# Moving two kinds of weight load from SyncE's queue to GpSimd's, with new places and delays, in a one-core decoder layer

## The chip, the cores and the metric

One core of a Trainium2 chip runs the whole kernel in one launch. The metric is the device time in microseconds (us), lower being better. TensorE multiplies matrices, VectorE (DVE) and ScalarE (ACT) do elementwise work, GpSimd (POOL) does a few small things here, and SyncE (SP) asks for most transfers. Each engine works through its own instructions in order. A DMA can be asked for on SP's queue or on POOL's; those that add to what lies at their destination are asked for on POOL's.

## The reference

A decoder layer over 256 tokens of width 2048 in float32:

```python
hn = rmsnorm(h, norm_mix_w)
q, k, v, g_ret, xr, yr, g_a, g_b = split(hn @ w_in)            # 2048 x 14336
ret_out = silu(g_ret) * head_groupnorm(chunkwise_retention(rotary(q), rotary(k), v))
rnn_out = gelu(yr) * rg_lru(causal_dwconv(xr))
merged = sigmoid(g_a) * (ret_out @ w_proj_ret) + sigmoid(g_b) * (rnn_out @ w_proj_rnn)
h = h + merged @ w_mix_out
h = h + memory_cross_attention(rmsnorm(h), rmsnorm(mem), w_q, w_k, w_v, w_o)
h = h + (silu(gate) * val) @ w_down        # gate, val = causal_dwconv(rmsnorm(h) @ w_up), 2 x 5632
out = rmsnorm(h, final_norm_w)
```

## The kernel before

**Products.** Every product is made in parts: a float32 operand is split into a high part, rounded to a shorter format that TensorE takes at full pace, and a low part, the rest. A product is then three matmuls, high x high, low x high and high x low. The high part of a weight is a ScalarE copy (`weight_parts`, L451), the low part a VectorE subtraction (L452).

**The weight stream.** The host lays all weights in one array in the order of use, and the kernel walks it piece by piece (`weight_stream`, 358 pieces, numbered by `i`). `plan` lists the weight products in order. A plain one covers 512 output columns, with a piece of four 128-row blocks. A pair covers two times 512 columns, with a piece of two row blocks by two column blocks (1 MB). `prefetch` loads a piece on SP into one of three buffers `raw` and splits it; `AHEAD = 2` keeps two pieces prepared ahead of the one in TensorE. `chunks` hands out a piece, counts a step per piece, and then runs the work that `later(n, fn)` put off by n steps.

**Kinds of pieces in a pair.** `MARKS` names for each pair the places (0 to 7, two row blocks each) that are treated in another way than the plain two-by-two product (kind 0). The numbers in a pair's tuple mean: 1 to 9, and 20s by their last digit, use seven block products instead of eight (Strassen's scheme, `steps_pair`), for which sums of the weight blocks and of the activations are needed; 20s also have their weight sums begun by DMA; -11 to -17 have lower parts of half of the piece (place 1 to 7) made by DMA, and -1 to -9 those of the whole piece.
- Kind 1, seven products: `seven_parts` makes the weight sums on VectorE with one addition of 1024 columns and two of 512 (L473).
- Kind 4, seven products with double loads: `load_twice` asks for one block twice into a tile `tw`, `add_to` lets a DMA on POOL's queue add two other blocks to it (L330), and `seven_loaded` has two VectorE additions of 512 columns left (L337).
- Kinds 2 and 3, far pieces: `request` loads blocks into a tile `fr`, `subtract` has ScalarE write their negation, rounded, into `fl` (L319) and a DMA on POOL's queue add the float32 block to it (L320), so that VectorE has no subtraction for these; kind 3 does so for half of the piece.

`LAG` says how many pieces ahead these begin: `far_load=3` and `sum_load=4` for the loads, 0 for ScalarE's negation and the additions; and how many steps other work is put off: `gelu` for the step from a transposed block to gelu (`gelu_y`), `rnn` and `rnn_step` for the activation sums of `w_proj_rnn`, `heads` for the split of the retention heads, `two_heads` for the heads' transposes, `residual` for squares, `key_turn` for the second pair of key blocks in the attention.

**Order.** Matmuls are kept in program order. For the other instructions a scheduler orders each engine's instructions by program order and by when their inputs are expected; it also gives out the 31 buffers of the pool `big`, in which `tw`, `fr`, `fl` and most activations live. An instruction waits in its engine's queue until its inputs are there and its buffer is free, and what is behind it on that engine waits too.

**Transposes.** Row blocks are turned into column blocks by DMA transposes asked for on SP (`by_dma`), followed `wait` steps later by ScalarE copies that join the halves (L677) and by whatever comes next.

Of the kernel before, what the change touches and what calls it, by code (L numbers as in the profile page):

```python
# [17 lines left out]
P = 128  # L18
D = 2048
S = 256  # L20
NT = D // P
# [5 lines left out]
FF = 5632  # L27
NF = FF // P
BW = 512
KC = 4  # L30
KH = 2
# [3 lines left out]
WARM = 7  # L35
FREE = 300
LAG = dict(
    sums=3, two_heads=3, recur=3, gelu=6, merged=4, memory=1, memory_step=4, rnn=2, rnn_step=2,
    heads=2, heads_step=1, squares=2, squares_step=1, rows=17, rows_step=2, residual=5, gate=2,
    value=4, merge_turn=1, query_turn=2, key_turn=3, turn=3, attend=3, acc_m=0, acc_h=0,  # L40
    by_rotate=0, by_conv=0, by_gelu=1, by_attend=1, far=0, far_load=3, sum_load=4, sum_add=0,
)
EPS = 1e-6
GN_EPS = 1e-5
# [1 line left out]
EARLY = [2, 2, 4, 4, 4]  # L46
MARKS = [
# [11 lines left out]
O_Q, O_K, O_V, O_G = 0, 1024, 2048, 4096  # L59
O_XR, O_YR, O_GA, O_GB = 6144, 8192, 10240, 12288  # L60
# [139 lines left out]
def hybrid_layer(  # L200
# [17 lines left out]
    act, dve, pe, pool, sp = nc.scalar, nc.vector, nc.tensor, nc.gpsimd, nc.sync  # L218
# [15 lines left out]
    def big(shape, dt=F32, s="b"):  # L234
        return bp.tile(shape, dt, tag="big", name=nm(s))
# [19 lines left out]
    def load(out, in_, pin):  # L255
        i = sp.dma_start(out=out, in_=in_)
        if pin:
            tc.keep_in_program_order(i)
# [43 lines left out]
    def source(i):  # L302

        _, _, nk, c = stream[i]
        return wall[at[i - 1] : at[i]].rearrange("(p k n) -> p k n", p=P, k=2 * nk if isinstance(c, tuple) else nk)

    def request(i):

        far[i] = []
        for k in (0, KH)[: 2 if stream[i][3][2] == 2 else 1]:  # L310
            raw = big([P, KH, BW], s="fr")
            load(raw, source(i)[:, k : k + KH, :], False)
            far[i].append(raw)

    def subtract(i):
# [7 lines left out]
    def load_twice(i):  # L323

        far[i] = t = big([P, KH, BW], s="tw")
        load(t, source(i)[:, 3:4, :].to_broadcast([P, KH, BW]), False)

    def add_to(i):

# [210 lines left out]
    def gemm_n(*args):  # L540
        return ended(steps_n(*args))
# [98 lines left out]
    def pair(*args):  # L640
        return ended(steps_pair(*args))

    def paired():

        return isinstance(plan[gemms[0]][3], tuple)
# [280 lines left out]
    for g in range(2):  # L926
        dec = big([P, 4, S], s="dec")
        vs, turned = [], ([], [])
        for b, o in enumerate((O_Q, O_K)):

            def rotate_both(f, o=turned[b]):
                o.append(rotated(f[:, 0:2, :]))
                later(0, lambda: o.append(rotated(f[:, 2:4, :])))

            v = None
            if b and not g and paired():
                a, v = pair("w_in", 0, xs, NT, O_K, O_V + BW)
                scaled(a, rs0)
                by_dma(a, rotate_both)
            else:  # L940
                a = gemm_n("w_in", 0, xs, NT, o + g * BW) if g + b else q0
                turned_rows(a, rs0, rotate_both, 2 - b if g + b else 3, g + b > 0, LAG["by_rotate"])
            if b == 1:
                sp.dma_start(
                    out=dec,
                    in_=consts[:, C_DEC + g * 4 * S : C_DEC + (g + 1) * 4 * S].rearrange("p (h s) -> p h s", s=S),
                )
            if g == 0:
                if v is None:
                    v = gemm_n("w_in", 0, xs, NT, O_V + b * BW) if b else ended(v_steps)  # L950
                vs.append(split_rows(v, rs0))
        if g == 1:
            vs += [split_rows(v, rs0) for v in pair("w_in", 0, xs, NT, O_V + 1024, O_V + 1024 + BW)]
        qr, kr = turned
        gates = []
        c = O_G + g * 1024
        for a in pair("w_in", 0, xs, NT, c, c + BW):
            t = big([P, 2, BW], s="gate")
            for tt in range(2):
                act.activation(t[:, tt, :], a[:, tt, :], AF.Silu, scale=rs0[:, tt : tt + 1])  # L960
            gates.append(t)
        retain(g, qr, kr, vs, dec, gates)
# [137 lines left out]
    def turn_merged(f):  # L1100
        for pr in range(2):
# [6 lines left out]
            if len(merged) == 2:  # L1108
                for k2 in range(NT // 2):
                    later(LAG["memory"] + LAG["memory_step"] * k2, lambda k2=k2: ms[k2])  # L1110

    ts, mb = [], []
    for b in range(2):
        ts.append(tanh_rows(big([P, 2, BW], s="sig"), gemm_n("w_in", 0, xs, NT, O_GB + b * BW)))
# [2 lines left out]
                later(LAG["rnn"] + LAG["rnn_step"] * i, lambda k2=k2: sums_of(rnn[k2]))  # L1117
    for b in (0, 2):
        if b:
            ts = [tanh_rows(a, a) for a in pair("w_in", 0, xs, NT, O_GB + b * BW, O_GB + (b + 1) * BW)]  # L1120
        for t, z in zip(ts, pair("w_proj_rnn", 0, rnn, NT, b * BW, (b + 1) * BW)):
            gated(t, z)
            mb.append(z)
# [3 lines left out]
        later(LAG["squares"] + LAG["squares_step"] * c, lambda c=c: memory_squares(c))  # L1127
    ts = []
    for b in (0, 2):
        ts += [tanh_rows(a, a) for a in pair("w_in", 0, xs, NT, O_GA + b * BW, O_GA + (b + 1) * BW)]  # L1130
    later(3, memory_begun)
    for b in range(4):
        later(LAG["rows"] + LAG["rows_step"] * b, lambda b=b: hrow.append(load_rows(x, b)))
# [169 lines left out]
    def down(b0, hid, n):  # L1303

        for b in (0, 2):
            for i, z in enumerate(pair("ffn_w_down", b0 * BW, hid, n, b * BW, (b + 1) * BW)):
                pool.dma_start(out=hrow[b + i], in_=z, accum_op=ALU.add)

    def down_final(b0, hid, n):
# [85 lines left out]
    def up(b, hid, seven, wait):  # L1395

        gt, vl = (big([P, 4, S], s=a) for a in ("fg", "fv"))

        def by_two(fn):
            fn(0)  # L1400
            if b < NF // 4 - 1:
                later(0, lambda: fn(1))
            else:
                fn(1)

        def gate(f):
            by_two(lambda pr: conv(f, 4 * b, gt, pr))

        def value(f):

            def both(pr):
                conv(f, NF + 4 * b, vl, pr)
                gate_up(gt, vl, hid, seven, pr)

            by_two(both)

        two = pair("ffn_w_up", 0, h2s, NT, b * BW, FF + b * BW)
        for a, then, wait in zip(two, (gate, value), (LAG["gate"], wait)):
            with tc.high_priority(FREE):
                for tt in range(2):  # L1420
                    act.mul(a[:, tt, :], a[:, tt, :], rs2[:, tt : tt + 1])  # L1421
            by_dma(a, then, wait)
# [58 lines left out]
```

## Time and profile before

| | before |
|---|---|
| median of 3 runs | 1954.9 us (1953.95 to 1956.12) |
| profiled execution, its own time | 1956.59 us |
| its span, first to last instruction | 1954.5 us |
| granted TensorE clock, mean | 0.999 |
| HBM read | 407.27 MB |
| packets of SP's queue, share of 16 engines' span | 66.5% |
| packets of POOL's queue, the same | 6.3% |

The profiled execution is one run; its span goes from the first instruction to the last, and its own time is somewhat longer. PE is TensorE's matmuls, PEld its weight loads beside them. A "SPq" or "POOLq" is the queue part of an engine: it asks for DMAs. In lists of groups the columns are busy us and mean ns of one, then the idle time before them and what ended it.

### The profile page before, as it was taken

To read this page: it belongs to the slowest core of one execution; us is meant where nothing else is said; L and a number is where in the kernel's file an instruction comes from. 1 tells how busy PE (TensorE), PEld (TensorE's weight loads), DVE (VectorE), ACT (ScalarE), POOL (GpSimd) and SP (SyncE) were. 2 spreads that over 40 slices of the span, in tenths; PEclk is the share of its full clock that TensorE was granted. 3 is DMA by queue.
4 is the path that set the end of the run, shared out by engine and by line. 5 is a ranking of instruction groups with operands and counts; after the bars stand their busy time and mean duration, and the time that the engine had idled before them with its cause. 6 is when DMAs were issued, how large, how long until landed. Compare 5 with 4: busy or idle time off the path is not lost.

```text
span 1954.5 us, 24287 instructions
## 1 busy us (share of the span) xinstructions
PE 1944.4 (99%) x8735; PEld 1612.9 (83%) x8735; DVE 1659.0 (85%) x2155; ACT 1457.7 (75%) x1792; POOL 68.5 (4%) x69
## 2 busy tenths in 40 slices
PE   9999999999999999999999999999999999999998
PEld 7888888888888888888888888888887888888887
DVE  6887987787889988887888857789999889999986
ACT  6665758999756666778678777888877578884784
POOL 0000001000100000000000000000000000000000
PEclk9999999999999999999999999999999999999999
DMA  8866767666867786778868687676677877678773
GB/s 332 262 215 198 245 222 217 213 218 229 237 217 265 233 264 215 253 253 252 247 213 239 223 221 225 226 232 226 211 224 224 269 248 221 223 224 271 230 255 119
DMA packets 211352, 454.99 MB, mean 233 GB/s; under 512 B 143264, under 2 KB 147872, under 8 KB 170400
## 3 DMA queue, kind: packets, MB, share of 16 engines
q1 hardware_dynamic: 204896, 430.38, 66.5%
q0 software_dynamic: 6336, 23.07, 6.3%
q8 instruction: 68, 1.11, 0.2%
q14 instruction: 52, 0.43, 0.1%
HBM read 407.27 MB, written 2.10 MB: 209 GB/s over the span
## 4 chain that ended last, share of the span: by engine, by line
PE 88%; DVE 5%; ACT 3%; DMA 2%; issue 2%; POOL 0%; SPq 0%; POOLq 0%; DVEq 0%; ACTq 0%
PE acc L285 63%; PE sm L285 26%; DVE lo L452 2%; ACT hi L451 1%; DMA raw<-in_wall 1%; ACT f L677 1%; DVE o L627 1%; ACT pl L664 0%; DMA fl<-fr 0%; DVE o L638 0%; DMA pt<-pl 0%; DVE raw L473 0%; DVE fv L1282 0%; DVE fg L1282 0%; DVE s L702 0%
## 5 line engine op out<-in xcount | busy, mean ns | idle before, releaser
L452 DVE TENSOR_TENSOR lo<-raw,hi 128x1024 fp32r<-128x1024 f32 (+1 forms) x824 | 940.4, 1169 | 203.0 <-ACT hi L451 193.0
L285 PE MATMUL acc<-hi,s 128*128 128x512 f32 x3526 | 1081.5, 388 | 0.4 <-ACT s L727 0.2
L451 ACT CAST hi<-raw 128x1024 fp32r<-128x1024 f32 (+1 forms) x824 | 801.1, 1007 | 301.9 <-DMA raw<-in_wall 83.1
L285 PEld LDWEIGHTS acc<-hi,s 128*128 128x128 f32 x3526 | 659.5, 188 | 136.1 <-DVE s L728 0.6
L285 PE MATMUL acc<-lo,s 128*128 128x512 f32 x1727 | 669.7, 388 | 0.1
L285 PE MATMUL sm<-hi,s 128*128 128x512 f32 x1464 | 450.9, 389 | 0.0
L285 PEld LDWEIGHTS acc<-lo,s 128*128 128x128 f32 x1727 | 324.4, 188 | 68.6 <-DVE lo L452 2.1
L285 PEld LDWEIGHTS sm<-hi,s 128*128 128x128 f32 x1464 | 274.7, 188 | 57.2 <-ACT prob L1203 0.2
L285 PE MATMUL sm<-lo,s 128*128 128x512 f32 x720 | 280.3, 389 | 0.0
L677 ACT COPY f<-pt 128x1024 uint16<-128x1024 uint16 x128 | 166.8, 1353 | 10.0 <-DMA pt<-pl 10.0
L285 PEld LDWEIGHTS sm<-lo,s 128*128 128x128 f32 x720 | 135.2, 188 | 28.6 <-DVE lo L452 0.6
L285 PE MATMUL acc<-hi,ts 128*128 128x512 f32 x438 | 134.9, 389 | 0.0
L473 DVE TENSOR_TENSOR raw<-raw 128x1024 f32<-128x1024 f32 x147 | 127.1, 865 | 1.9
L285 PEld LDWEIGHTS acc<-hi,ts 128*128 128x128 f32 x438 | 82.2, 188 | 17.0
L285 PE MATMUL acc<-lo,ts 128*128 128x512 f32 x219 | 85.7, 391 | 0.7 <-DVE lo L452 0.6
L664 ACT COPY pl<-o 128x1024 uint16<-128x1024 uint16 x64 | 62.5, 1040 | 3.7 <-DVE o L638 2.8
L330 POOL DMA_DIRECT2D tw<-in_wall x24 | 21.4, 891 | 980.8 <-DMA tw<-in_wall 355.7
L285 PEld LDWEIGHTS acc<-lo,ts 128*128 128x128 f32 x219 | 41.1, 188 | 10.8 <-DVE lo L452 2.4
L664 ACT COPY pl<-rows 128x1024 uint16<-128x1024 uint16 x44 | 43.7, 1044 | 7.6 <-DVE rows L694 7.6
L1421 ACT ACTIVATE o<-o,ro 128x512 f32<-128x512 f32 x44 | 30.1, 718 | 23.9 <-DVE o L638 23.8
L638 DVE TENSOR_TENSOR o<-o,sm 128x512 f32<-128x512 f32 x64 | 42.2, 679 | 3.9 <-PE sm L285 3.9
L285 PE MATMUL sm<-hi,ts 128*128 128x512 f32 x146 | 45.0, 389 | 0.0
(197 smaller groups left out, 1321.2 us busy)
## 6 DMA issues: line engine op xcount, KB each, us to landing
raw<-in_wall SPq DMA_DIRECT2D x319, 1024.0 KB, 5.1
raw<-in_wall SPq DMA_DIRECT2D x24, 768.0 KB, 5.6
tw<-in_wall SPq DMA_DIRECT2D x24, 512.0 KB, 7.7
tw<-in_wall POOLq DMA_DIRECT2D x24, 512.0 KB, 7.3
raw<-in_wall SPq DMA_DIRECT2D x13, 512.0 KB, 6.6
fr<-in_wall SPq DMA_DIRECT2D x12, 512.0 KB, 7.4
fl<-fr POOLq DMA_DIRECT2D x12, 512.0 KB, 8.1
nat<-in_x SPq DMA_DIRECT2D x8, 512.0 KB, 9.7
```

What stands on the lines that cost most here:

```text
L285: tc.keep_in_program_order(pe.matmul(*a, **k))
L330: pool.dma_start(out=far[i], in_=source(i)[:, 0:KH, :], accum_op=ALU.add)
L451: act.copy(hi[:, cs], src[:, cs])
L452: dve.tensor_tensor(out=lo[:, cs], in0=src[:, cs], in1=hi[:, cs].bitcast(F32), op=ALU.subtract)
L473: dve.tensor_tensor(out=o, in0=a, in1=b, op=ALU.add)
L627: dve.tensor_tensor(out=o, in0=a, in1=b, op=op)
L638: dve.tensor_tensor(out=o, in0=o, in1=a, op=ALU.add)
L664: act.copy(planes[:, tt], words[:, tt])
L677: act.copy(halves_[:, :, :, cs], turned_[:, :, :, cs])
L1421: act.mul(a[:, tt, :], a[:, tt, :], rs2[:, tt : tt + 1])
```

## The change

The loads of `request` and `load_twice` are asked for on POOL's queue instead of SP's. In `MARKS`, the pair `w_proj_rnn` columns 0 to 1023 has place 3 (piece 93) no longer with double loads but with VectorE's sums, and place 5 (piece 95) without a part made by DMA; the pair `w_in` for the gate `g_b`, columns 1024 to 2047, has place 7 (piece 105) without one. Several delays are set anew. A helper `blocks` gives a pair's two blocks as `pair` does, or two plain products where a pair has no seven; it takes the place of `pair` in five places.

```diff
 LAG = dict(
-    sums=3, two_heads=3, recur=3, gelu=6, merged=4, memory=1, memory_step=4, rnn=2, rnn_step=2,
-    heads=2, heads_step=1, squares=2, squares_step=1, rows=17, rows_step=2, residual=5, gate=2,
-    value=4, merge_turn=1, query_turn=2, key_turn=3, turn=3, attend=3, acc_m=0, acc_h=0,
-    by_rotate=0, by_conv=0, by_gelu=1, by_attend=1, far=0, far_load=3, sum_load=4, sum_add=0,
+    sums=3, two_heads=2, recur=3, gelu=7, merged=4, memory=1, memory_step=4, rnn=3, rnn_step=1,
+    heads=3, heads_step=2, squares=2, squares_step=1, rows=17, rows_step=2, residual=4, gate=2,
+    value=4, merge_turn=1, query_turn=2, key_turn=5, turn=3, attend=3, acc_m=0, acc_h=0,
+    by_rotate=0, by_conv=0, by_gelu=3, by_attend=2, far=0, far_load=3, sum_load=4, sum_add=0,
+    by_up=1,
 )
 MARKS = [
...
-    ((22, 23, 24, -16, -15, -11), (2, 5, 6, -17, -11), (2, 3, 5),),
+    ((3, 22, 24, -16, -11), (2, 5, 6, -11), (2, 3, 5),),
...
     def request(i):
...
-            load(raw, source(i)[:, k : k + KH, :], False)
+            pool.dma_start(out=raw, in_=source(i)[:, k : k + KH, :])
...
     def load_twice(i):
         far[i] = t = big([P, KH, BW], s="tw")
-        load(t, source(i)[:, 3:4, :].to_broadcast([P, KH, BW]), False)
+        pool.dma_start(out=t, in_=source(i)[:, 3:4, :].to_broadcast([P, KH, BW]))
...
+    def blocks(w, row, st, nk, c1, c2):
+        if paired():
+            yield from ((a, True) for a in pair(w, row, st, nk, c1, c2))
+        else:
+            for c in (c1, c2):
+                yield gemm_n(w, row, st, nk, c), False
...
-        two = pair("ffn_w_up", 0, h2s, NT, b * BW, FF + b * BW)
-        for a, then, wait in zip(two, (gate, value), (LAG["gate"], wait)):
+        two = blocks("ffn_w_up", 0, h2s, NT, b * BW, FF + b * BW)
+        for (a, own), then, wait in zip(two, (gate, value), (LAG["gate"], wait)):
+            if not own:
+                turned_rows(a, rs2, then, wait, by=LAG["by_up"])
+                continue
```

More of the change, by code (lines that the diff above doesn't have):

```diff
@@ L952, in hybrid_layer @@
         if g == 1:
-            vs += [split_rows(v, rs0) for v in pair("w_in", 0, xs, NT, O_V + 1024, O_V + 1024 + BW)]
+            vs += [split_rows(v, rs0) for v, _ in blocks("w_in", 0, xs, NT, O_V + 1024, O_V + 1024 + BW)]
         qr, kr = turned
@@ L956, in hybrid_layer @@
         c = O_G + g * 1024
-        for a in pair("w_in", 0, xs, NT, c, c + BW):
+        for a, _ in blocks("w_in", 0, xs, NT, c, c + BW):
             t = big([P, 2, BW], s="gate")
@@ L1110, in turn_merged, with tanhs @@
                     later(LAG["memory"] + LAG["memory_step"] * k2, lambda k2=k2: ms[k2])
+    def tanhs(c):
+        for a, own in blocks("w_in", 0, xs, NT, c, c + BW):
+            yield tanh_rows(a if own else big([P, 2, BW], s="sig"), a)
     ts, mb = [], []
@@ L1119, in hybrid_layer @@
         if b:
-            ts = [tanh_rows(a, a) for a in pair("w_in", 0, xs, NT, O_GB + b * BW, O_GB + (b + 1) * BW)]
+            ts = list(tanhs(O_GB + b * BW))
         for t, z in zip(ts, pair("w_proj_rnn", 0, rnn, NT, b * BW, (b + 1) * BW)):
@@ L1129, in hybrid_layer @@
     for b in (0, 2):
-        ts += [tanh_rows(a, a) for a in pair("w_in", 0, xs, NT, O_GA + b * BW, O_GA + (b + 1) * BW)]
+        ts += tanhs(O_GA + b * BW)
     later(3, memory_begun)
@@ L1305, in down @@
         for b in (0, 2):
-            for i, z in enumerate(pair("ffn_w_down", b0 * BW, hid, n, b * BW, (b + 1) * BW)):
+            for i, (z, own) in enumerate(blocks("ffn_w_down", b0 * BW, hid, n, b * BW, (b + 1) * BW)):
+                if not own:
+                    a, z = z, big([P, 2, BW], s="o")
+                    with tc.high_priority(FREE):
+                        act.copy(z, a)
                 pool.dma_start(out=hrow[b + i], in_=z, accum_op=ALU.add)
@@ L1415, in value @@
             by_two(both)
-        two = pair("ffn_w_up", 0, h2s, NT, b * BW, FF + b * BW)
-        for a, then, wait in zip(two, (gate, value), (LAG["gate"], wait)):
+        two = blocks("ffn_w_up", 0, h2s, NT, b * BW, FF + b * BW)
+        for (a, own), then, wait in zip(two, (gate, value), (LAG["gate"], wait)):
+            if not own:
+                turned_rows(a, rs2, then, wait, by=LAG["by_up"])
+                continue
             with tc.high_priority(FREE):
```

## The prediction, made before the change was run

> **What bounds the kernel now.** I read the page's first part, then the stretches of 50 us with TensorE's matmul counts, then the chain of work that ended last, and only then the queues that the change touches.
>
> ```profile
> span 1954.5 us, 24287 instructions
> PE 1944.4 (99%) x8735; PEld 1612.9 (83%) x8735; DVE 1659.0 (85%) x2155; ACT 1457.7 (75%) x1792; POOL 68.5 (4%) x69
> 1108.24 54.43 PE acc L285 x240
> 500.00:550.00 50.00, 49.37 (x219) 1.00 0.86 260
> 550.00:600.00 50.00, 50.00 (x222) 1.00 0.55 193
> 800.00:850.00 50.00, 49.87 (x220) 1.00 0.80 260
> 1450.00:1500.00 50.00, 49.53 (x214) 1.00 0.69 217
> 1500.00:1550.00 50.00, 49.62 (x218) 1.00 0.80 260
> ```
>
> TensorE is busy 99% of the span. A busy share alone could hide stalls, so I take the pace: the third line, from the chain, has 240 products in 54.43 us with nothing between them, 0.2268 us each. At that pace 50 us hold 220 starts, and a stretch counts one or two more that lie over its edges: 222 is a full stretch (second column: us, third: PE busy, in brackets the matmuls). Four stretches in the middle are short by 3, 2, 8 and 4 matmuls, 17 x 0.2268 = 3.9 us together. That is all that this change could win back, for it touches neither the first loads nor the last product, and it leaves every product in place: in all the pairs the set of second-level positions that use seven products instead of eight is the same before and after (the order in the tuple differs in one). 3.9 us is 0.2% of the time, about what a measurement of this kernel can tell from no change. The kernel is at its floor: the question is whether the change brings new gaps, not how much work it saves.
>
> **The change part by part.** First the calls. `blocks` yields what `pair` yields wherever a pair's marks name a seven, and all pairs that now go through it have one, so it and `by_up` change nothing. `by_gelu` and `by_attend` are only asked whether they are zero, so 3 for 1 and 2 for 1 change nothing.
>
> Second, the loads that move from SP to POOL.
>
> ```profile
> tw<-in_wall SPq DMA_DIRECT2D x24, 512.0 KB, 7.7
> tw<-in_wall POOLq DMA_DIRECT2D x24, 512.0 KB, 7.3
> fr<-in_wall SPq DMA_DIRECT2D x12, 512.0 KB, 7.4
> fl<-fr POOLq DMA_DIRECT2D x12, 512.0 KB, 8.1
> L256 SPq DMA_DIRECT2D tw<-in_wall x24: 378/426/1374, 81.5 to 1793.2; - x24
> L330 POOL DMA_DIRECT2D tw<-in_wall x24: 865/880/1054, 89.1 to 1799.7; - x24
> L256 SPq DMA_DIRECT2D fr<-in_wall x12: 327/382/1139, 214.6 to 1263.7; - x12
> SPq L256 <- DVE lo L452: 1209.9, 300, 11.9
> ```
>
> The first four lines give size and time to landing, the next three the least, median and most ns of one issue. SP loses 24 x 0.426 + 12 x 0.382 = 14.8 us of issuing. None of it is on the path: SP stood 1209.9 us waiting for VectorE's split to free a weight buffer (last line), and the waits, not the issues, place the weight loads. POOL gets 23 double loads and 10 far loads (one and two fewer, from the marks). A load on POOL is not in this trace; the nearest row is POOL's own 0.88 us for the accumulating load of the same tile and size, which lands after 7.3 us against SP's 7.7, so 33 x 0.88 = 29 us on an engine that is busy 4%. Bounds for one: 0.4 us earlier to 0.5 us later (0.880 less 0.382). The cover is the lead. A double load is asked for four pieces ahead of the preparation and the preparation runs two pieces ahead of the products: six pieces of about 5.2 us, 31 us, against 7.7 + 7.3 for load and addition. I cost the move at nothing, with 13 us or more to spare for a double load after the split's 1 to 2 us.
>
> The far loads have less: three plus two pieces, 26 us, against 7.4 for the load, 1.06 for ScalarE's negation and 8.1 for the addition, 17 us. 9 us are left. This is where POOL's order counts: an addition waits on POOL for its load to land or for ScalarE, and now the next load can stand behind it, where SP used to send it past.
>
> Third, the places. Two pieces (numbered by the order of the weight stream: 95 and 105) stop having lower parts made by DMA; piece 93 makes its weight sums on VectorE alone again.
>
> ```profile
> L452 DVE TENSOR_TENSOR lo<-raw,hi 128x1024 fp32r<-128x1024 f32 x745 | 889.4, 1220 | 199.5 <-ACT hi L451 189.7 <-PE acc L285 4.2 <-PE sm L285 2.1
> L473 DVE TENSOR_TENSOR raw<-raw 128x1024 f32<-128x1024 f32 x49 | 59.8, 1219 | 0.5
> L319 ACT ACTIVATE fl<-fr 128x1024 fp32r<-128x1024 f32 x12 | 12.6, 1056 | 0.0
> 500.00:520.00 20.00, 19.37 (x86) 15.73 (x85) 16.33 (x28) 12.30 (x16) 1.75 (x2) 1.00 0.88 263
> 520.00:540.00 20.00, 20.00 (x89) 16.54 (x89) 16.37 (x20) 14.76 (x17) 1.74 (x2) 1.00 0.80 223
> 560.00:580.00 20.00, 20.00 (x90) 16.57 (x89) 17.85 (x22) 12.42 (x14) 0.87 (x1) 1.00 0.61 202
> 580.00:600.00 20.00, 20.00 (x90) 16.57 (x89) 19.06 (x25) 13.55 (x17) 0.15 (x1) 1.00 0.62 236
> ```
>
> Each far piece given up returns one subtraction of 1.22 us to VectorE and takes 1.06 us from ScalarE and one addition from POOL; piece 93 takes one addition of 1024 columns back, 1.22 us. VectorE +3.66 us, ScalarE -2.1 us. In the window rows the busy times run PE, PE load, DVE, ACT, POOL. For 93 and 95 VectorE has 3.7 us idle in each 20 us (16.33, 16.37), against 2.44 in all; 105 is prepared at about 575, where 2.15 and 0.94 us are idle, against 1.22. On the path: nothing, with 0 to 3.7 us as the bounds.
>
> Fourth, the delays. The one with a gap next to it is `gelu` 6 to 7.
>
> ```profile
> 491.05 2.56 ACT L677 COPY f<-pt 128x1024 uint16<-128x1024 uint16 x2
> 494.93 1.06 ACT L1066 ACTIVATE f<-f 128x1024 f32<-128x1024 f32 x1
> 497.79 1.14 ACT L701 CAST s<-rn 128x512 fp32r<-128x512 f32 x2
> 499.50 1.29 DVE s L702 x2
> 503.16 0.97 ACT fl L319
> 504.52 8.56 DMA fl<-fr
> 513.12 2.56 PE acc L285 x10
> PE acc L285 <- DMA fl<-fr: 0.6, 1, 0.6
> 504.52 0.88 POOL L320 DMA_DIRECT2D fl<-fr  x1 [10.34 <-ACT fl L319]
> 518.47 0.87 POOL L320 DMA_DIRECT2D fl<-fr  x1 [13.08 <-ACT fl L319]
> ```
>
> This is the short stretch at 512. TensorE waits for the lower part of piece 91, which landed 8.56 us after POOL asked at 504.52, and POOL stood idle 10.34 us for ScalarE's negation. Ahead of it in program order ScalarE had the last gelu block (copies, table load, gelu, two casts, 491.05 to 498.9) and VectorE that block's split and the sums that ScalarE then waited for. One step later puts the gelu block behind the preparation of piece 91: a step is one piece, and the preparation of 91 falls in the step between. ScalarE then has about 6 us less in front of the negation, the addition can land before 513.1, and the gap goes: 0.63 us of PE idle, 3 matmuls by the count, 0.7 us. Next in line is that block's own output, wanted at pieces 96 and 97, five pieces later, with more than 20 us to spare. `rnn` and its step put the sums for piece 92 about one piece later, still some 6 us ahead of TensorE. The others (`two_heads`, `heads`, `residual`) move work inside leads of five pieces or more; I cost them at nothing. `key_turn` is a rival, below.
>
> The other short stretches (820, 1450 to 1540) are not reached by any delay. There SP loses one or two issues of 0.43 us; I credit nothing.
>
> **Sum.** The profiled execution took 1956.59 us for a span of 1954.5, 2.1 around it, and lies 1.7 above the median of the three runs, 1954.9. 1956.6 - 0.7 = 1955.9 for that execution, so 1954.2 for the median. The case's own range is 1951.0 (all 3.9 us come back) to 1958.6 (the 3.7 us of VectorE's extra work all on the path): within 0.2% either way.
>
> **Rivals.** *Slower by POOL's order.* In the stretch around 500 us the code asks POOL, in this order, for load 91, load 92, load 94, negated addition 91, addition 92, load 96, addition 94, load 99, addition 96. Load 96 used to go out on SP; now it stands behind two waiting additions. For: POOL's two longest waits there are the quoted 10.34 and 13.08 us. One of them in front of a far load uses up its 9 us and leaves 1.3 us of gap, both leave 23.4 - 9 = 14.4. It decides from 9 us of waiting. Between those ends I take 8 us, half-way: 1963. Against: the additions' waits are mostly for ScalarE, which gets freer here.
>
> *Slower by the delay of the keys.* `key_turn` 3 to 5 joins and splits the second pair of keys two steps later.
>
> ```profile
> 1086.60 0.64 ACT L701 CAST s<-f 128x512 fp32r<-128x512 f32 x1
> 1102.49 5.75 PE sm L285 x48
> 1080.00:1100.00 20.00, 20.00 (x89) 16.42 (x89) 20.00 (x23) 16.87 (x21) 0.00 (x0) 1.00 0.69 262
> ```
>
> The last split began at 1086.6; two pieces, 10.4 us, put it at 1097, its VectorE half at about 1098. The 48 products are the two logits, so those keys are wanted half-way, at 1105.4: 7 us left of 18. But VectorE is busy all of 1080 to 1100 and the products behind it wait as well. From 7 us of backlog on it opens a gap: behind the weight splits of two more pieces (10.4 us) it is 3.4 us, behind three 8.6; the middle, 6, gives 1960. Against: the same work leaves room in 1070 to 1087.
>
> *Slower by starved issues.* If POOL could write its requests only while VectorE is idle (3.7 of 20 us at 500), 0.88 us would become 4.8; five issues in front of load 96 are then 19.4 us late, 10 more than the lead: 1965. The rows speak against it: with VectorE busy 85%, POOL's issues took 865 to 1054 ns. The Trainium skill, SBUF — State Buffer, section "SBUF: two separate sides", has such a rule: requests from GpSimd's queue are written by GpSimd through a port pair that VectorE locks in its two-port modes, and it advises the hardware queues instead. It gives about 620 ns alone against 3100 beside a VectorE copy; by that, five issues are an estimated 12 us late and the time about 3 us longer. This trace shows no such issue, and VectorE's work here is two-input arithmetic almost throughout.
>
> *Faster beyond 0.2%.* SP, rid of 14.8 us of issues, sends the weight loads earlier and all four short stretches close: 1951 or just below.
>
> ```profile
> 1445.14 6.93 DMA raw<-in_wall
> 1474.13 5.88 DMA raw<-in_wall
> ```
>
> For: these two, from the chain, stand before the short stretch at 1450 to 1500. Against: what the loads waited for was a free buffer, not an issue.
>
> **How the numbers follow.** Forecast (the 512 gap goes, nothing else opens) 0.52; POOL's order 0.24; keys 0.15; starved issues 0.03; all gaps closed 0.06. So faster by over 0.2% is 0.06, within 0.2% is 0.52, slower by over 0.2% is 0.42. The range runs from 1951.0 to 1965.0, which takes in the middle of each slower case; what is left out, some 0.15 to 0.2, is the upper half of POOL's order and the little below 1951.
>
> **What would show it.** Right: a stretch 500 to 550 with 222 matmuls and no PE wait for fl; 23 double and 10 far loads under POOLq at about 0.9 us each; VectorE's busy time up by some 3.7 us, ScalarE's down by 2. Wrong: matmul counts below 222 anywhere new; in 500 to 550 with POOL idle in front of far loads (POOL's order), around 1105 with TensorE waiting for a key's split (keys), or POOL issues of several us (starved). Far off would be a change in the matmuls' number, or a gap at a place that I did not weigh, through buffers freed in another order.

## The result, and the profile after

The changed kernel is slower: 1968.9 us, median of 7 runs (1964.9 to 1980.29), against 1954.97 for the kernel before in the same session, a ratio of 1.0076 with a 95% interval of 1.0063 to 1.0088. The forecast was 1954.2 and its range ended at 1965.0.

The profiled execution of the changed kernel took 1980.29 us for a span of 1978.5. It is the longest of the seven, so what it shows is at the upper end of what this kernel does. These are the first lines of its page and of its queues.

```profile
span 1978.5 us, 24282 instructions
PE 1949.3 (99%) x8735; PEld 1613.0 (82%) x8735; DVE 1660.8 (84%) x2158; ACT 1452.5 (73%) x1790; POOL 86.9 (4%) x99
tw<-in_wall POOLq DMA_DIRECT2D x46, 512.0 KB, 7.5
fr<-in_wall POOLq DMA_DIRECT2D x10, 512.0 KB, 5.5
```

The matmuls are the same 8735. The 46 requests for `tw` are 23 double loads and 23 additions. The stretches of 50 us come next, with the columns as in the prediction, so the matmuls are in brackets and the last three numbers are the granted clock, the DMA share and GB/s.

```profile
500.00:550.00 50.00, 50.00 (x222) 1.00 0.68 221
650.00:700.00 50.00, 48.12 (x210) 1.00 0.60 212
800.00:850.00 50.00, 50.00 (x222) 1.00 0.79 263
1100.00:1150.00 50.00, 50.00 (x245) 1.00 0.76 227
1150.00:1200.00 50.00, 34.69 (x142) 0.83 0.84 126
1450.00:1500.00 50.00, 49.49 (x214) 1.00 0.80 232
1500.00:1550.00 50.00, 49.80 (x218) 1.00 0.72 230
```

The stretch at 500 is full now. One stretch is new and large: 1150 to 1200 has 80 matmuls less than a full 222, which at 0.2268 us each is 18.1 us. In it the DMA engines are busier (0.84) than in the other stretches shown and move 126 GB/s against their 212 to 263. A smaller hole is at 650 (12 matmuls, 2.7 us). TensorE's waits name the large one, in total us, times and longest:

```profile
PE acc L286 <- ACT ps L1254: 12.6, 1, 12.6
PE acc L286 <- DVE lo L453: 2.7, 6, 0.8
PE acc L286 <- DVE ps L1255: 2.7, 1, 2.7
```

`ps` is the split of the attention's probabilities (L1254 its high part on ScalarE, L1255 its low part on VectorE), which the next attention product needs. The wait for `fl` is gone from this list. The chain of work around the hole shows what stood ahead of `ps`:

```profile
1119.92 34.01 PE acc L286 x150
...
1154.34 23.70 DMA pt<-pl
1178.04 0.02 issue
1178.06 1.34 ACT f L686
...
1187.70 0.61 DVE ps L1255
1188.31 0.04 issue
1188.35 5.03 PE acc L286 x13
```

A DMA transpose of the attention's rows, asked for at 1154.34, landed 23.7 us later. The last line adds something: 13 products took 5.03 us, 0.387 each instead of 0.2268, 2.1 us more. The granted clock of that stretch is 0.83 in the mean, and from 1180 to 1192 it is 0.50. So 15.3 us of waiting and 2.1 us of slow products make up most of the hole of 18.1.

ScalarE's timeline shows the link from the transpose to `ps` (start, us, what, and in brackets the idle time before it and what ended it):

```profile
1169.37 1.35 ACT L686 COPY f<-pt 128x1024 uint16<-128x1024 uint16 x1 [9.42 <-DMA pt<-pl]
1178.06 1.33 ACT L686 COPY f<-pt 128x1024 uint16<-128x1024 uint16 x1 [7.34 <-DMA pt<-pl]
...
1183.80 0.62 ACT L1254 CAST ps<-f 128x512 fp32r<-128x512 f32 x1
```

The two copies that join the halves wait 9.42 and 7.34 us for the two transposes, and everything behind them on ScalarE waits too, `ps` last. Before, the same two copies began at 1158.84 without a wait and `ps` at 1165.81.

What ran beside those transposes? First the kernel before, POOL's timeline of 1140 to 1185 and then SP's:

```profile
1142.28 0.87 POOL L330 DMA_DIRECT2D tw<-in_wall  x1 [83.67 <-DMA tw<-in_wall]
1161.85 0.89 POOL L330 DMA_DIRECT2D tw<-in_wall  x1 [18.70 <-ACT f L677]
1167.27 0.88 POOL L330 DMA_DIRECT2D tw<-in_wall  x1 [4.54 <-ACT v L716]
```

```profile
1151.58 5.16 SPq L665 DMA_TRANSPOSE pt<-pl  x2
1156.79 0.58 SPq L256 DMA_DIRECT2D tw<-in_wall  x1
1158.75 0.33 SPq L256 DMA_DIRECT2D raw<-in_wall  x1
1159.24 0.38 SPq L256 DMA_DIRECT2D tw<-in_wall  x1
```

Then the changed kernel, the same two views (x2 is two issues in a row, with the time from the first to the last one's end):

```profile
1141.92 0.74 POOL L327 DMA_DIRECT2D tw<-in_wall  x1 [28.13 <-PE acc L286]
1147.75 0.87 POOL L331 DMA_DIRECT2D tw<-in_wall  x1 [5.09 <-DMA tw<-in_wall]
1149.98 0.76 POOL L327 DMA_DIRECT2D tw<-in_wall  x1 [1.36 <-ACT s L710]
1155.72 0.86 POOL L331 DMA_DIRECT2D tw<-in_wall  x1 [4.98 <-DMA tw<-in_wall]
```

```profile
1152.57 8.07 SPq L674 DMA_TRANSPOSE pt<-pl  x2
```

In POOL's views L331 (L330 before) is an addition and L327 a double load. They come in the order of the pieces of the pair `xa_w_o`, 212, 215 and 216; 1142.28 before is 212's addition, and the views after begin with 215. Before, SP's one queue put the double loads of 215 and 216 behind the pair of transposes (1151.58, then 1156.79 and 1159.24), and so their additions came after the pair had landed. After the change both go out on POOL ahead of the pair: 215 at 1141.92 with its addition at 1147.75, and 216 at 1149.98 with its addition at 1155.72, in the middle of the pair. The pair and this addition land late: the transposes after 16.8 and 23.7 us, the addition after 22.9. The load of 216 itself landed in time, after 5.4 us. Over the whole kernel the landing of a transpose (least, median, most) was 3.0, 3.3 and 7.7 us before; the view of the tile `pt` after has:

```profile
DMA to landing us min/median/max: 3.0/3.8/23.7
```

### The profile page after: what moved, and what is told of

Its sections match the earlier page's. It is cut to its first block, busy times and chain, and to the rows that moved or that the text cites. A ratio compares the mean times of both kernels' runs of the same rounds, so it can differ in the third digit from the quotient of the medians.

```text
span 1978.5 us, 24282 instructions
## 1 busy us (share of the span) xinstructions
PE 1949.3 (99%) x8735; PEld 1613.0 (82%) x8735; DVE 1660.8 (84%) x2158; ACT 1452.5 (73%) x1790; POOL 86.9 (4%) x99
## 4 chain that ended last, share of the span: by engine, by line
PE 89%; DMA 3%; DVE 3%; ACT 2%; issue 1%; POOL 0%; SPq 0%; POOLq 0%; DVEq 0%; ACTq 0%
PE acc L286 62%; PE sm L286 27%; DMA pt<-pl 2%; DMA raw<-in_wall 1%; DVE lo L453 1%; ACT hi L452 1%; ACT f L686 0%; ACT pl L673 0%; DVE s L711 0%; DVE fv L1296 0%; DVE raw L474 0%; DVE tb L858 0%; ACT rows L926 0%; DMA raw<-in_head 0%; ACT fg L1294 0%
## 5 line engine op out<-in xcount | busy, mean ns | idle before, releaser
L628 DVE TENSOR_TENSOR o<-o,acc 128x512 f32<-128x512 f32 x64 | 43.6, 681 | 0.5
```

The costliest lines, as they stand in the source:

```text
L628: dve.tensor_tensor(out=o, in0=a, in1=b, op=op)
```

## The experiments

All times are medians with the range of the runs, and each ratio is against the kernel before, run in the same session on the same chip.

**Which part of the change costs.** The first: the changed kernel with both kinds of load back on SP, so that only places and delays differ from before.

```diff
 def request(i):
-            pool.dma_start(out=raw, in_=source(i)[:, k : k + KH, :])
+            load(raw, source(i)[:, k : k + KH, :], False)
 def load_twice(i):
-        pool.dma_start(out=t, in_=source(i)[:, 3:4, :].to_broadcast([P, KH, BW]))
+        load(t, source(i)[:, 3:4, :].to_broadcast([P, KH, BW]), False)
```

> The changed kernel with both kinds of loads asked for on SP again; its places and delays stay. Theory Q (the loads on POOL's queue cost it): the time falls to 1953 to 1956, no transposed block lands later than about 10 us, no gap of TensorE over 2 us in the middle. Theory D (the new delays and places cost it): 1963 to 1975 as with the change, with the gap before the attention's last blocks near 1171 us.

Measured: 1956.08 (1954.9 to 1958.42), ratio 1.0001 (0.9991 to 1.001). Two of its 50 us stretches, for comparison with those above:

```profile
650.00:700.00 50.00, 50.00 (x222) 1.00 0.67 213
1150.00:1200.00 50.00, 50.00 (x222) 1.00 0.76 212
```

Both holes are gone. The second run is the opposite: the kernel before with these two lines changed as the diff of the change has them, and nothing else.

> The kernel before with both kinds of loads asked for on POOL; its places and delays stay. Theory Q: slower by 8 us or more, 1963 to 1975, with transposes or additions that land after 15 us or more somewhere. Theory D: 1953 to 1957.

Measured: 1968.79 (1957.79 to 1972.22), ratio 1.006 (1.0041 to 1.0078); TensorE waits 4.9 and 2.7 us for `ps`. The third has only the double loads back on SP (the second half of the diff above), with the far loads on POOL.

> The changed kernel with only the double loads back on SP, the far loads left on POOL. Theory Q with the double loads as the part that counts (256 descriptors of 2 KB, 23 of them): 1953 to 1957. If the far loads count: 1960 or more. Theory D: 1963 to 1975.

Measured: 1957.21 (1954.89 to 1959.65), ratio 1.0006 (0.9997 to 1.0016). The fourth is the changed kernel again, unaltered.

> The changed kernel unchanged, for a second profile of it. If its extra time is one fixed gap (the attention blocks at 1171 us, 15 us of idle TensorE), the gap is there again in the same place. If it is a collision of transfers that depends on small shifts, the large gap is elsewhere, of another size, or absent, and the times spread over 1963 to 1980 again.

Measured: 1969.7 (1968.97 to 1971.68), ratio 1.0071 (1.0056 to 1.0086). Its waits show that the hole is in the same place but varies in size from one execution to the next, so neither theory holds as it stood:

```profile
PE acc L286 <- DVE ps L1255: 3.1, 1, 3.1
...
PE acc L286 <- ACT ps L1254: 1.7, 1, 1.7
```

What follows: places and delays cost and gain nothing that can be measured, the far loads on POOL about 1 us, which is within the noise, and the double loads on POOL nearly all of it.

**Which double loads.** The changed kernel has 23: 3 in `xa_w_o`, 6 in the feed-forward products, 14 elsewhere. First the three of `xa_w_o` go back to SP.

```diff
-        pool.dma_start(out=t, in_=source(i)[:, 3:4, :].to_broadcast([P, KH, BW]))
+        (sp if stream[i][0] == "xa_w_o" else pool).dma_start(out=t, in_=source(i)[:, 3:4, :].to_broadcast([P, KH, BW]))
```

> The changed kernel with the double loads of one pair alone (xa_w_o, pieces 212, 215, 216) back on SP, the other 20 left on POOL. Theory P (one place: there POOL sends a double load and its addition past the transposes of the attention's rows, which on SP stood ahead of the load): the gap near 1170 us goes and the time falls by 7 to 10 us, to 1958 to 1962. Theory W (every double load on POOL costs a little): it falls by 3 of 23 parts, 2 us.

Measured: 1963.95 (1962.1 to 1968.61), ratio 1.0046 (1.0031 to 1.0061), and no wait for `ps`. The fall of some 5 us lies between the two theories. Then those of the feed-forward products as well (`or stream[i][0].startswith("ffn")` added to the condition).

> The changed kernel with the double loads of xa_w_o and of the feed-forward products (11 of 23) on SP, 12 left on POOL. If what is left beside the gap at 1170 us lies in the feed-forward part (late weights at 1450 to 1560 us): 1956 to 1959. If it is spread over all: 1960 to 1962.

Measured: 1960.21 (1957.11 to 1963.29), ratio 1.0022 (1.0012 to 1.0031). By its trace this run has 9 double loads on SP and 14 on POOL; the expectation's 11 and 12 were miscounted. So the loss goes in steps: 1.0071 with all on POOL, 1.0046, 1.0022, 1.0006 with all double loads on SP, 1.0001 with the far loads there too. In us of 1955.4 the steps are 4.9, 4.7, 3.1 and 1.0; neighbouring intervals touch, so the order of size is not settled between the first three. The large hole is one of several meetings.

The other way round, the kernel before with only the three of `xa_w_o` on POOL (the same line, with `!=`):

> The kernel before with the double loads of xa_w_o alone asked for on POOL. Theory P: the gap near 1170 us appears, with transposes that land after 12 us or more, and the time rises by 6 to 10 us, to 1961 to 1965. Theory W: by 2 us.

Measured: ten runs in two groups, five of 1954.81 to 1957.39 and five of 1969.55 to 1972.7; ratio of the medians 1.0035 (1.001 to 1.0061). The median, 1963.47, is inside the expected range only because it lies between the groups. The profiled run is of the upper group. Its POOL timeline:

```profile
1140.40 0.75 POOL L326 DMA_DIRECT2D tw<-in_wall  x1 [26.61 <-DMA pt<-pl]
1146.34 0.88 POOL L330 DMA_DIRECT2D tw<-in_wall  x1 [5.19 <-DMA tw<-in_wall]
1149.70 0.74 POOL L326 DMA_DIRECT2D tw<-in_wall  x1 [2.48 <-ACT hi L451]
1154.85 0.90 POOL L330 DMA_DIRECT2D tw<-in_wall  x1 [4.40 <-DMA tw<-in_wall]
```

These are load and addition of piece 215, then of 216. The pair went out on SP from 1151.81, 216's addition at 1154.85 in the middle of it, and TensorE waited 9.3 + 2.7 us for `ps`. Three loads make the whole hole in a kernel that is otherwise the one before, and they make it all or nothing: about 15 us in half of the runs.

**Is it the loads themselves?** Two kernels without the layer, which only ask for these transfers again and again, with nothing else going on. The first puts a pair of transposes behind one other transfer, or two.

```python
sections = (
    lambda i: [turned(i)],
    lambda i: [twice(sp, i), turned(i)],
    lambda i: [twice(pool, i), turned(i)],
    lambda i: [added(i), turned(i)],
    ...
)
```

> Not the layer: a pair of DMA transposes of the kernel's size, twelve times each alone and just behind a double load on SP, a double load on POOL, an addition on POOL, a 1 MB weight load on SP, and that weight load with each of the three; then each of the three alone. If a transfer on POOL's queue as such slows transposes (theory Q): the second transpose of the pair lands 2 us or more later behind a double load on POOL than behind one on SP. If only the moment counts, that is that SP used to hold the load back behind the transposes (theory P): the same within 1 us. If additions are what jams: the section with weight load and addition has transposes of 10 us and more.

Measured, medians from the first request of a pair to its last landing: alone 4.43 us, behind a double load of SP 5.76, of POOL 6.57, behind an addition 6.88, with a 1 MB weight load as well 7.90, 8.02 and 8.16; the longest of all 9.18. A double load on POOL is 0.8 us worse for the pair than one on SP, which is within theory P's 1 us, and nothing comes near 20 us. An addition that is asked for ahead of the pair does not jam it here.

The second has the kernel's sequence: weight load, pair, weight load on SP, and a double load with its addition, which waits for it.

```python
def chain(engine, i, first, add=True, second=True):
    ...
    if first:
        made.append(twice(engine, i))
    made.append(raw(i))
    made.append(turned(i))
    ...
    if add:
        add_to(made[0 if first else 2], i)
```

> Not the layer: the transfers around the gap at 1170 us by themselves, 24 times each: a weight load, a pair of transposes and another weight load on SP, with a double load on POOL or SP ahead of the pair or behind it and its addition on POOL once it has landed. Theory J (two POOL transfers, the load's end and the addition, that meet a pair of transposes jam them): in the sections with the double load ahead the pair's second transpose lands after 12 us or more in some of the 24, and with the load behind the pair never. Theory T (it needs the whole kernel's traffic): all pairs land within 9 us, and the sections differ by 1 to 2 us at most.

Measured, the same medians: double load ahead on POOL 6.6 (7.6 without the addition), ahead on SP 12.3 (9.7 without), behind the pair on SP 6.3. Asked for behind the pair on POOL, where nothing holds it back, the load in fact went out 1.2 us ahead of the pair: 7.8. With the load ahead on POOL the addition was asked for 5.0 us after the pair's first request, when the pair was nearly done (landings at 5.7 and 6.6). With the load ahead on SP it was asked for at 5.9, when the second transpose without an addition lands only at 9.7, and the two landed together at 12.3. So theory J's 12 us came in all 24 turns with the load ahead on SP and in none with it on POOL; a load ahead on SP delays the pair by itself, and an addition that starts inside the pair adds 2.6 us there. The 17 to 24 us of the layer are not reached.

**Moving the moment.** Three runs of the changed kernel. In the first, ScalarE's join of the attention's rows comes one step later, so that `ps` is no longer right behind it.

```diff
-        turned_rows(a, shares[b], lambda f: split_block(f, osp, marks_of("xa_w_o")), by=LAG["by_attend"])
+        turned_rows(a, shares[b], lambda f: split_block(f, osp, marks_of("xa_w_o")), 2, by=LAG["by_attend"])
```

> The changed kernel with the join of the attention's turned row blocks put off one step more (2 for 1). If the late transpose costs time because ScalarE's join of it stands in order ahead of the probabilities' copy that TensorE needs next, the wait for ps near 1170 us goes, though the transposes still land after 12 us or more, and the time falls by 6 to 10 us. If TensorE loses the time to late weights instead, it stays at 1966 to 1972.

Measured: 1970.48 (1962.46 to 1976.68), ratio 1.0068 (1.0048 to 1.0089). No better: TensorE still waited 5.1 us for `ps` in the profiled run. The remedy at the waiting end does not work. The second has the double loads one piece later (`sum_load=3`), on POOL.

> The changed kernel, loads on POOL, with every double load asked for one piece later (sum_load 3 for 4, some 5 us). Theory M (the moment counts: on POOL the loads go out ahead of the transposes and weight loads that SP kept in front of them): the gap at 1170 us goes or changes, and the time falls to 1957 to 1963. Theory Q (POOL's queue as such): 1966 to 1972 as with the change.

Measured: 1982.83 (1977.13 to 1988.31), ratio 1.0134 (1.0111 to 1.0158): slower than either theory said. The waits for `ps` are 11.3 + 2.7 us, and a transpose lands after 22.9 us at most; both additions, 215's and 216's, now start inside the pair. Later loads give other meetings, not fewer. The third has them one piece earlier (`sum_load=5`) and on SP.

> The loads on SP again and every double load asked for one piece earlier (sum_load 5 for 4). Theory M: a load that stands ahead of the transposes on SP costs as well, 1959 or more. Theory Q: 1954 to 1957, like the loads on SP with 4.

Measured: 1957.3 (1955.56 to 1959.34), ratio 1.0008 (0.9998 to 1.0017). This does not test theory M at the attention's pair: by the trace the loads of 215 and 216 went out at 1155.30 and 1156.43, still behind the pair on SP (1149.99).

**Holding POOL's requests.** Four runs on what decides at 1150 to 1190. The kernel before with the three loads of `xa_w_o` on POOL (the one with two groups), and one addition held: between the load and the addition of piece 215 POOL copies two elements of the rows that the attention's pair of transposes writes.

```diff
 def add_to(i):
+        if stream[i][0] == "xa_w_o" and stream[i][1] == 1280:
+            gate = sp_.tile([P, 2], U16, tag="gate", name=nm("gate"))
+            with tc.issue_after(loaded[i].ins):
+                behind_turn = pool.tensor_copy(gate, turns[-2][:, 0, 0, 127:129])
+            with tc.issue_after(behind_turn.ins):
+                pool.dma_start(out=far[i], in_=source(i)[:, 0:KH, :], accum_op=ALU.add)
+            return
         pool.dma_start(out=far[i], in_=source(i)[:, 0:KH, :], accum_op=ALU.add)
```

> The kernel before with the three double loads of xa_w_o on POOL (as in the run where the times fell into two groups, 1954.8 to 1957.4 and 1969.6 to 1972.7), and one addition held: POOL copies two elements of the attention's turned rows to a scratch tile between the load and the addition of piece 215, so that this addition can't start before those two transposes have landed. Theory S (an addition that starts while a pair of transposes is in flight makes both land late): the pair lands within 9 us, no wait of TensorE near 1170, all runs in 1954 to 1958. Theory Q (any double load on POOL beside the transposes does it, through its bytes or its queue): still two groups, the upper at 1970 or more.

Measured: 1957.02, all eleven runs within 1953.3 to 1957.66, ratio 1.0 (0.9991 to 1.0008). No run is in the upper group. The run with two groups was of another session and chip, so this sets 0 of 11 against 5 of 10 across sessions. POOL's timeline, SP's, and the landing of the transposes from 1140 to 1192:

```profile
1156.82 0.42 POOL L335 COPY gate<-pt 128x2 uint16<-128x2 uint16 x1 [17.92 <-DMA pt<-pl]
1157.38 0.88 POOL L337 DMA_DIRECT2D tw<-in_wall  x1
1158.22 0.80 POOL L326 DMA_DIRECT2D tw<-in_wall  x1
1167.01 0.90 POOL L339 DMA_DIRECT2D tw<-in_wall  x1 [7.99 <-DMA tw<-in_wall]
```

```profile
1149.44 5.21 SPq L675 DMA_TRANSPOSE pt<-pl  x2
```

```profile
DMA to landing us min/median/max: 4.0/5.2/6.4
```

The landing went from 20.4 us at most to 6.4. But the hold moves more than one addition, since what stands behind the copy on POOL waits with it. The addition of 215 goes from 1146.34 to 1157.38, and the load and the addition of 216, the two that had met the pair (1149.70 and 1154.85), go to 1158.22 and 1167.01. The load of 215 had landed at 1144.40, 5 us before the pair was asked for. So the run shows that the hole goes when POOL's requests stay clear of the pair. It does not part the load of 216 from its addition, as it was meant to do with 215's. The next run holds the load of 215 as well, with the copy ahead of it.

> As the first, but the copy stands ahead of the load of piece 215 on POOL, so that load and addition both start after the two transposes have landed. Theory S and theory Q: 1954 to 1958, all runs in one group. If this is in one group and the run with only the addition held is in two, the load does it. If neither is in one group, POOL's queue as such is at fault, or another piece.

Measured: 1957.7 (1955.89 to 1961.39), ratio 1.0008 (0.9999 to 1.0017). Holding the load of 215 (now at 1159.06) adds nothing; 216 is behind the pair in both runs. The next has one double load only, that of piece 215, on POOL.

```diff
-        load(t, source(i)[:, 3:4, :].to_broadcast([P, KH, BW]), False)
+        (pool if stream[i][0] == "xa_w_o" and stream[i][1] == 1280 else sp).dma_start(out=t, in_=source(i)[:, 3:4, :].to_broadcast([P, KH, BW]))
```

> The kernel before with one single double load, that of piece 215, on POOL; all other loads on SP. Theory S: one load is enough, since its addition then starts beside the pair: two groups, 1954 to 1958 and 1966 to 1973. If it needs the other two loads as well (more bytes on POOL): one group, 1954 to 1957.

Measured: 1959.29 (1955.89 to 1964.57), ratio 1.0012 (1.0003 to 1.0021), one group and barely clear of the noise. The two groups that the theory expected did not come. The profiled run's POOL timeline, with the load and the addition of 215, says why:

```profile
1142.18 0.77 POOL L326 DMA_DIRECT2D tw<-in_wall  x1
1150.39 0.88 POOL L330 DMA_DIRECT2D tw<-in_wall  x1 [7.44 <-DMA tw<-in_wall]
```

In the two-group run it was 216 whose load and addition met the pair. Here 216's load is on SP again and goes out behind the pair, at 1158.79. The addition of 215 started 0.3 us before the pair was asked for (1150.69). The pair's transposes then took 9.0 and 7.6 us and TensorE waited 0.9. So 215 alone does not make the large hole, and an addition already in flight cost little in this execution.

Last, the changed kernel with the same hold; 216's load and addition again come behind it (1165.66 and 1174.05).

> The changed kernel with the same one addition (piece 215) held behind the attention's transposes, all loads on POOL. Theory S: the gap of TensorE near 1171 goes, the smaller gaps elsewhere (650, 1450 to 1560) stay, 1961 to 1965. Theory Q: 1968 to 1971 as without it.

Measured: 1966.32 (1963.53 to 1969.59), ratio 1.0048 (1.0035 to 1.006). There is no wait for `ps` left; the median is above the expected 1961 to 1965. In the median this one place is worth about 3 to 5 us (1.0071 to 1.0048 here, to 1.0046 with the three loads on SP). The remaining 9 us is spread, as the waits of its profiled run show:

```profile
PE acc L286 <- DVE lo L462: 3.2, 6, 1.2
PE sm L286 <- DVE o L648: 2.3, 2, 2.1
```

The first line is of weight splits that came late. The hole at 650 in the changed kernel reads so: POOL sends two double loads (631.14, 639.40) and two additions (640.54, 643.82) around three weight loads, which land after 9.8 to 11.1 us; with the loads on SP weight loads there land after 4.7 to 6.9. That these meetings make the small holes is read from the trace and from the ladder above; none of them was held by itself.

## Why the prediction was wrong

**Right in its parts.** The matmuls are unchanged. The hole at 512 went, as the delay of gelu was said to do: 222 matmuls from 500 to 550, no wait for `fl`. With the loads on SP it is gone too, so the queue did not do it; the delay was not tried without the new places. VectorE has 3 instructions more and ScalarE 2 fewer, as counted; in time it is +1.8 and -5.2 us against the forecast +3.66 and -2.1, and none of it shows on the path. The 33 loads go out on POOL at medians of 0.752 us (double) and 0.556 (far), below the 0.88 taken and inside the bounds given. The sum of all this, no measurable change, is what the run with places and delays alone gave: 1.0001.

**The step that failed.** It is "I cost the move at nothing, with 13 us or more to spare". The working asked whether a load that goes out on POOL lands in time, and it does. It did not ask what the load and its addition would land beside. On SP a double load stood in one order with the weight loads and the transposes, behind whatever had been asked for before it; on POOL it goes out as soon as its buffer is free and POOL's previous request is done, 9 us earlier for piece 216 (1149.98 against 1159.24) and 29 near 650 (639.40 against 668.07 with the loads on SP), and its addition follows it. On SP the order of one queue had kept the requests of 215 and 216 behind the attention's pair. That protection was removed with the 14.8 us of issues, and was priced at zero. What stood in its place: waits of 5 to 15 us for `ps` in all six profiled executions in which the addition of 216 starts inside the attention's pair, and some 9 us in smaller meetings.

That the hole comes from POOL's double loads and their additions meeting this pair is shown by the runs that moved or held them. Which of 216's two requests does it stays open. The traces point at the addition: in the six executions the load of 216 had landed 10 us or more before the second transpose did, and the addition landed within 0.9 us of that transpose. But an addition inside a pair is not enough by itself: in four of the six traces the addition of 215 started inside the previous pair, around 1146, and no transpose of that pair took over 5 us.

The lead of 31 us covered the load's own consumer. It did not cover that of the transposes, ScalarE's join with `ps` behind it, and the working had no line for that, because it followed only what waits for POOL.

**The rivals.** *POOL's order* had the right queue and sign and half the price (1963), and failed in place and mechanism: it looked at far loads around 500, held behind waiting additions. Those stretches are full, and far loads on POOL cost about 1 us, within the noise. The loss comes from what POOL's requests meet, not from requests held behind waiting additions. *Keys' delay*: 1100 to 1150 has TensorE busy 50.00 of 50, so it costs nothing. *Starved issues*: POOL's double loads took 717 to 1087 ns with VectorE busy 84%, so none took the several us of this rival. The 3.1 us that the Trainium skill's page SBUF — State Buffer, section "SBUF: two separate sides", has for a GpSimd DMA beside a VectorE copy does not appear in these requests. *All gaps closed*: with places and delays alone, the loads on SP, the gaps at 500 and 820 closed and the one at 1450 nearly (221 matmuls), but 1500 to 1550 still has 219 and 1750 to 1800 has 216 where it had 222 before, and the median did not move measurably.

**What would have shown it.** The trace before had both halves: the row of 1151.58 with the double loads right behind it on SP, and POOL's additions at 1161.85 and 1167.27, after the pair had landed. Only one addition in it starts inside a transpose, at 170.44, half a us before that transpose landed, so the price could not be read there. That alone was a reason to widen the range: a meeting that the trace hardly shows had been bounded at 0.5 us.

The Trainium skill, DMA: Bandwidth & Descriptors, section "Issuing engines are not separate DMA queues", says that transfers of all issuing engines run on the same 16 DMA engines and that starting them from several engines saves only the time of starting them. The first half is in keeping with this trace, where requests of the two queues slow each other (transposes of SP 23.7 us, an addition of POOL 22.9); the saving here was worth less than the order that it gave up, 0.6% (0.41 to 0.78%) in the kernel before with nothing but the queue changed.

## What to carry to other kernels

A queue is also an order: when a transfer moves to another queue, list what it used to stand behind, and look where it and what it releases will now run, above all beside transfers with an in-order consumer. Price it by the neighbours it will have as well as by its own lead. If the move is wanted for other reasons, hold its requests behind the transfer that they disturb: with a copy of two elements on POOL, 0.42 us, no run had the hole, where the same three loads without it had cost 15 us in half of the runs. What stands behind the copy on POOL waits with it.

## What the runs showed of the hardware

- DMA transposes land later beside POOL's transfers. Over the sixteen traces of the layer, worked out from request and landing times: mean 4.23 us with no POOL transfer beside it (1765 cases, longest 9.0), 5.52 beside a POOL load (126, longest 9.6), 5.79 with an addition already in flight (79, longest 12.9), 7.60 with an addition that starts before it lands (78, longest 23.7). A transpose that is late for another reason gives an addition more time to start in it, so the last mean is too high as a price.
- Seven transposes took over 13 us, all in the attention's pair of 1150 to 1160, and in each an addition had started 0.3 to 3.2 us after the request. Three more of that pair, with an addition inside them as early, took 8.7 to 12.8 us. But nine others at other places had an addition start as early and landed in 3.2 to 4.6 us. One difference can be read in all six jammed pairs: the 1 MB weight load asked for ahead of the pair had 2.6 to 7.3 us still to go when the addition started; in the nine, such a load had landed, was not there, or had 0.6 us to go. No run set this by itself, so that a jam needs the transposes, the addition and this load together is not shown.
- In the packet records of the hole, 1160 to 1178, a transpose's 256 B packets took 122 ns in the mean and an addition's 4096 B packets 749, against 22 and 358 for the same two kinds in the trace before (1151 to 1160 and 1161 to 1172). The medians stay (18 and 327); about a tenth of the packets take over 340 and 2200 ns.
- By themselves, without the layer, the same transfers bring a pair to 12.8 us at most. What the layer adds was not found, nor why the hole comes in some executions of one kernel and not in others.
- DMA engines that are busy are not DMA engines at work: 0.84 busy at 126 GB/s in the hole, 0.76 at 212 in the same stretch without it.
- A hole costs more than its length: after 15.3 us of waiting the first 13 products ran at 0.387 us each, 2.1 us on top, with a granted clock of 0.50 from 1180 to 1192.
- A double load on POOL is issued in 0.75 us against 0.88 for the accumulating request of the same size.
- The same double load goes out as 256 packets of 2048 B on SP and as 128 of 4096 B on POOL, so the change of queue also changes the packets. With POOL's requests held behind the pair the packets were POOL's and the hole was gone, so they do not make it by themselves.
